# The lowest decay level of the HGRN scores, as products of neighbouring tokens summed by a matmul with ones

## The chip, the core and the metric

The kernel runs on one core of a Trainium2 chip, as one program. The metric is the device time of one execution in microseconds (us); the median of several runs counts. Engines are named as in the profile: TensorE (PE, its weight loads PEld), VectorE (DVE), ScalarE (ACT), GpSimd (POOL) and SyncE (SP), whose queue issues the DMAs.

## What is computed

The reference is one decoder layer over 512 tokens of 1024 channels, all in float32: a SwiGLU feed-forward network, a token mixer, and a second feed-forward network, each between two norms and with a residual. The mixer has four heads of HGRN2 and four of mLSTM. The change touches the scores of the HGRN heads. For one head with 128 channels, a query q, a key k = 1 - f and the logarithm of the forget gate f, the reference does, in each chunk:

```python
G = jnp.cumsum(gc, axis=2)
rel = G[:, :, :, None, :] - G[:, :, None, :, :]
decay = jnp.exp(jnp.where(causal, rel, -jnp.inf))
scores = jnp.sum(qc[:, :, :, None, :] * kc[:, :, None, :, :] * decay, axis=-1)
o = o_inter + jnp.einsum("bhts,bhsv->bhtv", scores, vc)
```

So the score of query t and key s is the sum over the channels of q_t k_s exp(G_t - G_s). For neighbours, t = s + 1, the decay is just f_t = 1 - k_t, and the score is the sum over the channels of q_t (1 - k_t) k_s.

## The kernel before

The tokens are held in four tiles of 128. The first feed-forward network runs, then the mixer, then the second network. TensorE does nearly all of its work in pieces that are queued so that something is always ready: in the mixer, `fill(n)` takes the next n steps of a queue of projections (`job_f` and `job_t`) and puts them between the steps of the HGRN and mLSTM parts. The projections multiply in a split form: each weight tile comes by DMA, ScalarE casts its high part (L208), VectorE makes the low part (L210), and three matmuls use them (L435, or L126 to L128).

Before the mixer's scores, `forget_gates` makes kk = 1 - f and the running sums G for two pairs of heads, `masks` lets GpSimd make the masks, the eye and the selectors, and ScalarE makes the queries q.

The scores are not made from the exponentials of G over a whole chunk, which would overflow, but by levels. `LEVELS` holds block sizes c = 1, 64, 32, 16, 8, 4, 2. At level c the 128 tokens of a chunk are cut into pairs of neighbouring blocks of c tokens; the queries of each second block meet the keys of the first. In `hgrn_level`, for c > 1, the queries are scaled by exp(G - ref) and the keys by exp(ref - G), with ref the G at the end of the first block (L996 to L1000). The scaled queries qe of the second blocks are packed to 512 columns for a pair of heads (2 heads of 4 chunks of 64 queries). For c = 1 no exponential is needed: L1002 makes 1 - kk of the odd tokens, that is f, and the keys are kk itself. L1005 multiplies the queries in. Then, at every level, eight matmuls (L1010), one for each head and chunk, take the 128 keys as weights and 64 columns of qe as the moving operand, and leave all scores of 128 keys by 64 queries in a PSUM bank. `copy_predicated` (L1014) takes from it the places that the level's mask allows, into sT.

`hgrn_levels` calls the levels for a pair of heads with their steps interleaved: level c = 1 comes first, before `hgrn_diag` (the scores of a token with itself, matmuls on L1050), then `hgrn_decays`, which takes the logarithm of kk in place (L958, so kk is used up) and makes H = G - log k there (L959), then the other levels. The keys of level c = 64, which is the second, need that H (L998, L1000). Pair 0 comes first, with six steps of the projections between two levels, then pair 1 with five, along with the gates of the mLSTM heads.

The order of the instructions on each engine is worked out when the program is built, by a planner that simulates the engines with durations of its own: it takes the earliest instruction in the program's order that is ready. On the chip each engine then goes through its queue in that order and waits where it must.

PSUM has eight banks, taken in turn by `ps()`; qe and the other work tiles of 512 columns come from four buffers (`st`).

Of the kernel before, what the change touches and what calls it, by code (L numbers as in the profile page):

```python
# [8 lines left out]
F32 = mybir.dt.float32  # L9
F32R = mybir.dt.float32r  # L10
AF = mybir.ActivationFunctionType
ALU = mybir.AluOpType
PSUM = bass.MemoryType.PSUM

P = 128
# [52 lines left out]
class Layer:  # L68
# [816 lines left out]
    def masks(self, mc, mb):  # L885

        nc = self.nc

        self.mask = mb.tile([P, len(LEVELS), 64], I32, name="mask")
        nc.gpsimd.memset(self.mask, 1)  # L890
        for n, c in enumerate(LEVELS):
            m = self.mask[:, n, :].rearrange("p (b c) -> p b c", c=c)
            pat = [[-2 * c, 64 // c], [0, c]]
            nc.gpsimd.affine_select(m, m, pattern=pat, compare_op=ALU.is_ge, fill=0.0, base=0, channel_multiplier=1)
            pat = [[2 * c, 64 // c], [0, c]]
            nc.gpsimd.affine_select(m, m, pattern=pat, compare_op=ALU.is_ge, fill=0.0, base=c - 1, channel_multiplier=-1)
        self.eye = mb.tile([P, P], I32, name="eye")
        nc.gpsimd.memset(self.eye, 1)
        nc.gpsimd.affine_select(
            self.eye, self.eye, pattern=[[1, P]], compare_op=ALU.is_equal, fill=0.0, base=0, channel_multiplier=-1  # L900
        )

        sel = mb.tile([4, 6, 2, 64], F32, tag="tmp", bufs=1, name="sel")
        nc.gpsimd.memset(sel, 1.0)
        self.sel = mc.tile([36, 6, P], F32R, name="selr")
        nc.gpsimd.memset(self.sel.bitcast(I32), 0)
        for n in range(6):
            pat = [[0, 2], [0, 64]] if n < 4 else [[-1, 2], [0, 64]]
            base = -n if n < 4 else -2 * (n - 4)
            nc.gpsimd.affine_select(  # L910
                sel[:, n], sel[:, n], pattern=pat, compare_op=ALU.is_equal, fill=0.0, base=base, channel_multiplier=1
            )
        for r in (0, 32):
            nc.gpsimd.tensor_copy(self.sel[r : r + 4], sel.rearrange("p n a b -> p n (a b)"))
# [69 lines left out]
    def hgrn_level(self, p, n, ke):  # L984

        nc = self.nc
        c = LEVELS[n]
        q, kk, G = self.q[p], self.kk[p], self.G[p]
        flat = lambda t: t.rearrange("p a t -> p (a t)")
        blk = lambda t: flat(t).rearrange("p (b two c) -> p b two c", two=2, c=c)  # L990
        qe = self.st("qe")
        qe3 = qe.rearrange("p (b c) -> p b c", c=c)
        if c > 1:
            el = self.st("el")
            el3 = el.rearrange("p (b c) -> p b c", c=c)
            ref = blk(G)[:, :, 0, c - 1 : c].broadcast_to([P, 512 // c, c])  # L996
            nc.vector.tensor_tensor(qe3, blk(G)[:, :, 1, :], ref, op=ALU.subtract)
            nc.vector.tensor_tensor(el3, ref, blk(kk)[:, :, 0, :], op=ALU.subtract)  # L998
            nc.scalar.activation(qe, qe, AF.Exp)
            nc.scalar.activation(blk(ke)[:, :, 0, :], el3, AF.Exp)  # L1000
        else:
            nc.vector.tensor_scalar(qe3, blk(kk)[:, :, 1, :], -1.0, 1.0, op0=ALU.mult, op1=ALU.add)  # L1002
            ke = kk
        yield
        nc.vector.tensor_tensor(qe3, qe3, blk(q)[:, :, 1, :], op=ALU.mult)  # L1005
        yield
        sc = self.ps()
        k8, q8 = flat(ke).rearrange("p (n s) -> p n s", s=P), qe.rearrange("p (n u) -> p n u", u=64)
        for m in range(8):
            nc.tensor.matmul(sc[:, 64 * m : 64 * m + 64], k8[:, m], q8[:, m], start=True, stop=True)  # L1010
        yield
        so = self.sT[:, 8 * p : 8 * p + 8, :].rearrange("p n (b two c) -> p n b two c", two=2, c=c)[:, :, :, 1, :]
        mk = self.mask[:, n : n + 1, :].broadcast_to([P, 8, 64]).rearrange("p n (b c) -> p n b c", c=c)
        nc.vector.copy_predicated(so, mk, sc.rearrange("p (n b c) -> p n b c", n=8, c=c))  # L1014
        yield
# [493 lines left out]
```

## Time and profile before

| what | value |
|---|---|
| median of 3 runs | 960.77 us (960.7 to 960.91) |
| the profiled execution | 960.65 us |
| its span, first to last instruction | 958.9 us |
| VectorE busy, 404 to 450 us | 37.83 of 46 us |
| VectorE busy, 450 to 457 us | 6.70 of 7 us |
| level c = 1, TensorE | from 400.8 us (pair 0) and from 454.2 us (pair 1) |

The profile is of one execution. Its page gives the busy time of each engine, the chain of waits that ended last and the costliest groups of instructions; further views give the instructions of one line, the instructions in order of time, and who waited for whom. In a timeline row stand the start in us, the duration in us, the engine, the line, the operation, what it writes and reads, and in brackets the idle time just before with what ended it. In a row of the chain in order of time stand the start, the duration, engine and tile, line, and a count. Matmuls overlap in the array, so the duration of one record is longer than the time by which the next one follows; the chain's rows give the latter.

### The profile page before, as it was taken

Reading aid. Unit: us, or ns where it says so; the run is one execution under the profiler, and the core shown is the slowest. Engines: PE = TensorE matmul, PEld = TensorE weight load, DVE = VectorE, ACT = ScalarE, POOL = GpSimd, SP = SyncE. Lnnn points to the kernel's source line nnn. Section 1 sums busy time; section 2 is a strip of 40 time slices with the busy share of each in tenths; the row PEclk is TensorE's granted clock in tenths of the full one; section 3 lists DMA queues with packets and bytes.
Section 4 is the critical chain, followed back from the end, with each engine's and each line's share of the span. In section 5 each row is a group of like instructions: output and inputs, shape, how many; then the busy total and the mean of one; then the engine's idle time right before and its main releaser. Section 6 shows DMA issues by size and latency. Waiting matters only on the chain.

```text
span 958.9 us, 15940 instructions
## 1 busy us (share of the span) xinstructions
PE 950.7 (99%) x6587; PEld 875.8 (91%) x6587; DVE 693.5 (72%) x860; ACT 467.2 (49%) x625; POOL 113.3 (12%) x160
## 2 busy tenths in 40 slices
PE   9999999999999999999999999999999999999997
PEld 7999999999888889998887888899999999988885
DVE  6799989987444476697846565797998899754543
ACT  7645444544434356855632444663454444543531
POOL 3530000000000035200001310344000000000001
PEclk9999999999999999999999999999999999999999
DMA  9244433244222024421312124324434332233202
GB/s 321 76 133 131 130 113 110 89 133 154 89 94 82 1 73 130 109 67 45 87 46 67 45 88 148 102 60 132 123 98 132 111 111 88 91 109 109 88 1 87
DMA packets 81666, 95.97 MB, mean 100 GB/s; under 512 B 4117, under 2 KB 61497, under 8 KB 81594
## 3 DMA queue, kind: packets, MB, share of 16 engines
q1 hardware_dynamic: 81306, 94.44, 31.7%
q8 instruction: 51, 0.84, 0.4%
q10 hardware_dynamic: 288, 0.52, 0.2%
q14 instruction: 21, 0.17, 0.1%
HBM read 92.85 MB, written 2.10 MB: 99 GB/s over the span
## 4 chain that ended last, share of the span: by engine, by line
PE 98%; issue 1%; ACT 0%; DMA 0%; POOL 0%; DVE 0%; DVEq 0%; POOLq 0%; ACTq 0%
PE ps L490 45%; PE ps L126 13%; PE ps L128 13%; PE ps L127 13%; PE ps L435 6%; PE ps L1010 3%; PE ps L269 1%; PE ps L445 1%; PE ps L1184 0%; PE ps L115 0%; PE ps L1095 0%; PE ps L1264 0%; PE ps L1291 0%; PE ps L1050 0%; PE ps L1288 0%
## 5 line engine op out<-in xcount | busy, mean ns | idle before, releaser
L208 ACT CAST w<-raw 128x1024 fp32r<-128x1024 f32 x214 | 225.3, 1054 | 322.8 <-PE ps L128 118.4
L210 DVE TENSOR_TENSOR w<-raw,w 128x1024 fp32r<-128x1024 f32 x214 | 268.9, 1259 | 123.6 <-ACT w L208 123.6
L490 PE MATMUL ps<-xq,w 128*128 128x256 f32 x2016 | 238.1, 277 | 0.0
L490 PEld LDWEIGHTS ps<-xq,w 128*128 128x128 f32 x2016 | 233.7, 188 | 0.2
L490 PE MATMUL ps<-sq,w 128*128 128x256 f32 x1440 | 171.0, 277 | 0.0
L490 PEld LDWEIGHTS ps<-sq,w 128*128 128x128 f32 x1440 | 167.4, 188 | 0.0
L128 PE MATMUL ps<-w,hs 128*128 128x512 f32 x336 | 131.0, 390 | 0.0
L126 PE MATMUL ps<-w,hs 128*128 128x512 f32 x336 | 130.9, 390 | 0.0
L127 PE MATMUL ps<-w,hs 128*128 128x512 f32 x336 | 130.8, 389 | 0.0
L126 PE MATMUL ps<-w,xq 128*128 128x512 f32 x208 | 84.9, 409 | 0.1
L128 PE MATMUL ps<-w,xq 128*128 128x512 f32 x208 | 81.1, 391 | 0.0
L127 PE MATMUL ps<-w,xq 128*128 128x512 f32 x208 | 81.1, 391 | 0.0
L224 DVE TENSOR_TENSOR raw<-raw,raw 128x1024 f32<-128x1024 f32 x64 | 80.0, 1251 | 0.7
L128 PEld LDWEIGHTS ps<-w,hs 128*128 128x128 f32 x336 | 63.1, 188 | 13.8 <-DVE hs L674 0.7
L127 PEld LDWEIGHTS ps<-w,hs 128*128 128x128 f32 x336 | 63.1, 188 | 12.8
L126 PEld LDWEIGHTS ps<-w,hs 128*128 128x128 f32 x336 | 63.1, 188 | 12.8
L356 POOL TENSOR_SCALAR col<-col 128x1 f32<-128x1 f32 x24 | 10.1, 422 | 500.6 <-ACT junk L355 500.4
L435 PE MATMUL ps<-xq,w 128*128 128x256 f32 x480 | 56.5, 278 | 0.0
L435 PEld LDWEIGHTS ps<-xq,w 128*128 128x128 f32 x480 | 55.5, 188 | 0.0
L674 DVE TENSOR_TENSOR hs<-hf,hs 128x1024 fp32r<-128x1024 f32 x42 | 51.2, 1218 | 0.0
L224 POOL TENSOR_TENSOR raw<-raw,raw 128x1024 f32<-128x1024 f32 x16 | 43.1, 2695 | 52.3 <-DVE w L210 43.0
L128 PEld LDWEIGHTS ps<-w,xq 128*128 128x128 f32 x208 | 39.0, 188 | 8.9 <-DVE xq L276 0.3
(231 smaller groups left out, 1015.4 us busy)
## 6 DMA issues: line engine op xcount, KB each, us to landing
raw<-in_ffn_w_in_dram SPq DMA_DIRECT2D x88, 512.0 KB, 4.4
raw<-in_ffn_w_out_dram SPq DMA_DIRECT2D x44, 512.0 KB, 3.8
raw<-in_w_mix_in_dram SPq DMA_DIRECT2D x28, 512.0 KB, 3.9
raw<-in_w_mix_out_dram SPq DMA_DIRECT2D x8, 512.0 KB, 3.7
out_dram<-xs SPq DMA_DIRECT2D x8, 256.0 KB, 2.1
xs<-in_x_dram SPq DMA_DIRECT2D x6, 256.0 KB, 6.4
gpost<-in_norm_post_dram SPq DMA_DIRECT2D x3, 512.0 KB
gpre<-in_norm_pre_dram SPq DMA_DIRECT2D x2, 512.0 KB, 4.1
```

Source lines behind the costliest of these rows:

```text
L126: mm(ps, sh, mh, start=start, stop=False, **kw)
L127: mm(ps, sh, ml, start=False, stop=False, **kw)
L128: mm(ps, sl, mh, start=False, stop=stop, **kw)
L208: nc.scalar.copy(hi, raw)
L210: nc.vector.tensor_tensor(lo, raw, hi.bitcast(F32), op=ALU.subtract)
L224: (nc.vector if late else nc.gpsimd).tensor_tensor(o, o, c, op=ALU.add)
L269: self.nc.tensor.transpose(pt[:, c * P : (c + 1) * P], src[:, k * P : (k + 1) * P], self.ident)
L356: nc.gpsimd.tensor_scalar(m, ss, s2 / D, b, op0=ALU.mult, op1=ALU.add)
L435: mm(ps[:, u0:u1], w[:, a, k, :], self.xop(k, b, u0, u1), start=k + n + m == 0, stop=k == ND - 1 and n == 2, skip_group_check=True,)
L490: self.nc.tensor.matmul(ps[:, c], wb[b][:, k, v], left[d][:, k, :], start=first and a + n + k == 0, stop=n == 2 and k == KH - 1, skip_grou ...
L674: self.nc.vector.tensor_tensor(t[:, 1], src, t[:, 0].bitcast(F32), op=ALU.subtract)
L1010: nc.tensor.matmul(sc[:, 64 * m : 64 * m + 64], k8[:, m], q8[:, m], start=True, stop=True)
```

## The change

For c = 1 alone, the packed queries are multiplied once more on VectorE, by the keys kk of the even tokens. Every column of qe then holds, for one pair of neighbours, the 128 channels' products q_t (1 - k_t) k_s. One matmul with a weight tile of ones sums them over the channels, and every one of the 128 output rows holds the same sum; the mask of the level takes the row that belongs to the key. The eight matmuls of this level go, for each of the two pairs, and so does the reading of kk by TensorE. The tile of ones is a new tile of 128 x 128, filled once by GpSimd ahead of the eye.

```diff
@@ masks
+        self.ones = mb.tile([P, P], F32, name="ones")
+        nc.gpsimd.memset(self.ones, 1.0)
         self.eye = mb.tile([P, P], I32, name="eye")
@@ hgrn_level
             nc.vector.tensor_scalar(qe3, blk(kk)[:, :, 1, :], -1.0, 1.0, op0=ALU.mult, op1=ALU.add)
-            ke = kk
         yield
         nc.vector.tensor_tensor(qe3, qe3, blk(q)[:, :, 1, :], op=ALU.mult)
+        if c == 1:
+            nc.vector.tensor_tensor(qe3, qe3, blk(kk)[:, :, 0, :], op=ALU.mult)
         yield
         sc = self.ps()
-        k8, q8 = flat(ke).rearrange("p (n s) -> p n s", s=P), qe.rearrange("p (n u) -> p n u", u=64)
-        for m in range(8):
-            nc.tensor.matmul(sc[:, 64 * m : 64 * m + 64], k8[:, m], q8[:, m], start=True, stop=True)
+        if c == 1:
+            nc.tensor.matmul(sc, self.ones, qe, start=True, stop=True)
+        else:
+            k8, q8 = flat(ke).rearrange("p (n s) -> p n s", s=P), qe.rearrange("p (n u) -> p n u", u=64)
+            for m in range(8):
+                nc.tensor.matmul(sc[:, 64 * m : 64 * m + 64], k8[:, m], q8[:, m], start=True, stop=True)
         yield
```

## The prediction

> **What bounds the kernel now.** I read the page's engine sums first, then the chain of waits, then what TensorE waited for.
>
> ```profile
> span 958.9 us, 15940 instructions
> PE 950.7 (99%) x6587; PEld 875.8 (91%) x6587; DVE 693.5 (72%) x860; ACT 467.2 (49%) x625; POOL 113.3 (12%) x160
> PE 98%; issue 1%; ACT 0%; DMA 0%; POOL 0%; DVE 0%; DVEq 0%; POOLq 0%; ACTq 0%
> PE ps L122 <- POOL ident masks.py:199: 1.5, 1, 1.5
> core 0: 958.9 us, clock 0.999
> ```
>
> TensorE is busy for 950.7 of 958.9 us, it makes up 98% of the chain that ended last, and the only wait of its matmuls that the view of waits shows is 1.5 us at the very start. So a stage's price is the time that its matmuls occupy TensorE, and work on the other engines is free until it makes TensorE wait. Of the 958.9 us only TensorE's can be saved by a change in the mixer.
>
> The change touches the lowest level (c = 1), once for each of the two head pairs. The chain in order of time shows both places, each between matmuls that fill TensorE around it:
>
> ```profile
> L1010 PE MATMUL ps<-qe,kk x32: 217/275/275, 400.8 to 455.8; 128*128 128x64 f32 x32
> 398.80 2.12 PE ps L435 x18
> 400.92 1.73 PE ps L1010 x16
> 402.65 10.65 PE ps L435 x90
> 451.20 1.78 PE ps L1050 x16
> 454.15 0.23 PE ps L128
> 454.38 1.73 PE ps L1010 x16
> 456.11 0.29 PE ps L126
> 456.40 0.23 PE ps L127
> ```
>
> The rows of L1010 that read kk are level c = 1: 8 matmuls of 64 columns in each pair, and 16 records, so an f32 matmul is recorded as two passes, each with its own weight load. One block takes 1.73 us. The first matmul after the block takes 0.29 instead of 0.23 us, so I count 1.73 + 0.06 = 1.79 us for the whole block, or 0.11 us a pass. L1050 just before it makes passes of 128 columns, and 16 of them take 1.78 us: 64 and 128 columns cost the same, 0.11 us. At this width the pass isn't bound by its columns but by the weight load beside it.
>
> **The change part by part.** *The matmuls.* Eight matmuls of 64 columns become one of 512 columns: the same 512 columns, but 2 weight loads in place of 16. A warm f32 pass of 512 columns is not in the trace. The nearest rows are these:
>
> ```profile
> 520.25 0.87 PE ps L1243 x4
> 521.12 0.23 PE ps L126
> L1243 PE MATMUL ps<-vm,kw 128*128 128x258 f32 x12 | 3.1, 380 | 0.0
> 2.87 3.78 PE ps L115 x4
> 8.22 1.89 PE ps L269 x8
> 21.24 0.87 PE ps L269 x8
> L115 PE MATMUL ps<-hf,one 1*128 1x512 f32 x4 | 3.8, 1096 | 0.1
> ```
>
> L1243 is f32 with 258 columns: 4 passes in 0.87 us, 0.2175 us each, twice the 0.11 us of 128 columns, so here the columns do decide, at 0.2175/258 = 0.84 ns a column. 512 columns give 0.43 us a pass, 0.86 us a matmul. The matmul behind L1243 takes its usual 0.23 us, so nothing is added at the exit. The second way to it is L115, an f32 matmul of 512 columns, but at the start of the program, where TensorE is slow: 3.78/4 = 0.945 us a pass. The same group of 8 transposes (L269) takes 1.89 us there and 0.87 us at 21 us; 0.945 x 0.87/1.89 = 0.435 us. Both ways agree on 0.43 us, and I take 0.86 us a matmul. The saving is 1.79 - 0.86 = 0.93 us a pair, **1.86 us** in both; if the 0.06 us at the exit stays, 1.74 us.
>
> The bounds of this price, by the rows however far: at worst the pass of L115 as it stands, 1.89 us a matmul, which is 0.10 us more than the block now, a loss of 0.2 us in all. At best the 0.23 us of L127, a pass of 512 columns of the other f32 type: 0.46 us a matmul, a gain of 2 x 1.33 = 2.66 us. I take 0.86 because L1243 has the same type, both operands of 128 partitions and a warm TensorE. The bounds give 958.1 and 961.0 us.
>
> The Trainium skill, page "TensorE: Matmul & The Clock Gate", Part 1, says that the array runs at half its clock until some 3.4 us of activity have passed. By that rule a pass of L115 would halve to 0.47 us and the saving would be 2 x (1.79 - 0.945) = 1.69 us, 959.1 us in all. The two rows of L269 agree with a halving (a factor of 2.2).
>
> *The products.* In each pair one more VectorE operation multiplies qe by every second column of kk. It has the shape and stride of the operation on L1005: 0.69 us, 2 x 0.69 = 1.4 us of VectorE time. It may run as soon as L1005 of this level is done:
>
> ```profile
> 390.76 0.69 DVE L1005 TENSOR_TENSOR qe<-qe,q 128x512 f32<-128x512 f32 x1 [0.69 <-ACT q L1365]
> 392.91 0.96 DVE L977 TENSOR_TENSOR qd<-q,qd 128x768 f32<-128x768 f32 x1 [1.47 <-ACT qd L964]
> 438.20 0.69 DVE L1005 TENSOR_TENSOR qe<-qe,q 128x512 f32<-128x512 f32 x1
> 440.43 0.71 DVE L1014 COPY_PREDICATED sT<-mask,ps 128x512 f32<-128x512 int32 x1 [1.54 <-PE ps L1010]
> ```
>
> In pair 0 VectorE is idle for 1.47 us behind it, in pair 1 for 1.54 us, and 0.69 us fits into either hole. The matmul of the level waits for the new product in place of the old one. That is ready at about 392.1 and 439.6 us, 8 and 14 us before TensorE reaches the place (400.9 and 454.4). So I cost it at nothing. Behind that matmul in TensorE's queue stand the projections (90 matmuls of L435 in pair 0), so a product later than that would stop all of TensorE. Without this cover it is 0.69 us in the chain of the next level, which is the first rival.
>
> *The ones.* GpSimd fills a tile of 128 x 128 ahead of the eye.
>
> ```profile
> masks.py:197 POOL MEMSET ident<- 128x128 f32 x1 | 0.2, 205 | 0.3 <-POOLq L1496 0.3
> 375.29 0.47 POOL L899 TENSOR_SCALAR_AFFINE_SELECT eye<-eye 128x128 int32<-128x128 int32 x1
> 386.47 0.73 POOL L904 MEMSET sel<- 4x768 f32 x1 [9.11 <-DVE G L946]
> ```
>
> The same fill costs 0.2 us at the start. What stands behind it in GpSimd's queue is late by 0.2 us: the rest of the masks and the eye, which is done at 375.8 us and first used after the matmuls of L1050 at about 397 us, then an idle stretch of 9.11 us. Nothing.
>
> *What is released.* The logarithm on L958 overwrites kk. Until now it had to wait for the matmuls of L1010, which read kk; afterwards only for those of L1050 and for a product long done:
>
> ```profile
> 402.73 1.28 ACT L958 ACT_TABLE_LOAD   x1 [1.38 <-PE ps L1010]
> 456.14 1.16 ACT L958 ACTIVATE kk<-kk,tiny 128x1024 f32<-128x1024 f32 x1 [0.58 <-PE ps L1010]
> 462.51 0.61 ACT L1000 ACTIVATE ke<-el 128x512 f32<-128x512 f32 x1
> 463.99 1.98 PEld L1010 LDWEIGHTS ps<-qe,ke 128*128 128x128 f32 x16
> 446.85 0.69 DVE L1005 TENSOR_TENSOR qe<-qe,q 128x512 f32<-128x512 f32 x1 [1.26 <-ACT qe L999]
> 461.07 1.22 DVE L210 TENSOR_TENSOR w<-raw,w 128x1024 fp32r<-128x1024 f32 x1
> ```
>
> ScalarE gets back up to 1.38 and 0.58 us of waiting. TensorE doesn't wait for it, so the gain is nothing, but it helps at the tightest place, which is level c = 64 of pair 1: its weights ke are ready at 462.51 + 0.61 = 463.1 us, and TensorE loads them at 463.99, a slack of 0.9 us. TensorE will come there 1.86 us earlier. Behind 446.85 us VectorE works without a break on what feeds ke; that backlog starts 0.93 us earlier, since it hangs on ScalarE's wait for TensorE behind pair 0. So 0.9 + 0.93 - 1.86 leaves about 0 us, and what L958 gains by its earlier release comes on top. I take no wait there.
>
> *The sum.* The profiled execution took 960.65 us, of which 958.9 are the span and 1.75 lie around it and stay. 960.65 - 1.86 = 958.79. The median of the runs, 960.77, lies 0.12 us higher: **958.9 us**.
>
> **The rivals.** *The next level comes too late.* If the order of work on VectorE puts the new product of pair 1 behind 446.85 us, into the stretch without a break, and that stretch doesn't move forward with TensorE, ke is late by 1.86 - 0.9 + 0.69 = 1.65 us, and the time is 960.55. For it speaks that the slack is small; against it the hole of 1.54 us at the product's natural place and ScalarE's earlier start.
>
> *Slower than before.* The order on each engine comes from a planner that sees other durations than before. If at the same place two splits of weights (L210, 1.22 us each) are also put ahead of what feeds ke, the delay is 1.65 + 2.44 = 4.1 us and the time 958.9 + 4.1 = 963.0. It decides from a delay of 1.86 us on, where the gain is gone. Against it: TensorE's order follows the program's here, and the splits have several buffers of cover.
>
> *The change doesn't save what it says.* If the weight loads had been hidden and only columns counted, equal columns would cost the same and nothing would be gained but the 0.12 us at the exits: 960.65, the same as 960.77. The equal price of passes of 64 and 128 columns speaks against it. The Trainium skill, same page, section "Back-to-back issue gap", counts an isolated matmul by its columns alone; the section adds that a stream of weight loads and matmuls is set by both, and the two rows, 1.73 and 1.78 us, side with that.
>
> *A cheaper pass.* At 0.23 us a pass the time is 958.1. Against it stands L1243.
>
> **How the numbers follow.** I call 0.2% (1.92 us, so 958.85 us) what a measurement can tell from no change. The forecast, with its own range of 958.7 to 959.1 (savings of 1.74 to 1.86 us, and 0.1 us to either side, since the runs lie between 960.7 and 960.91), gets 0.62. It lies on that border, and I divide it evenly. The late level gets 0.14, slower than before 0.10, nothing saved 0.05, the cheaper pass and anything else that gains 0.09. Faster by over 0.2%: 0.31 + 0.09 = 0.40, and 0.03 for smaller waits that close up around the blocks, taken from the even half: 0.43. Slower by over 0.2% (over 962.7): 0.08 of the 0.10. The rest, 0.49, is within 0.2%. The range goes from the cheaper pass to the dear one, 958.1 to 961.0, and leaves out the slower case and little else.
>
> **What would show it.** Two records of L1010 with 128x512 in each pair, about 0.43 us apart, where there were sixteen, 0.86 us for the block, and the matmul behind it at 0.23: if a pass takes 0.9 us, the price was wrong. Two more operations of VectorE at 0.69 us, inside the holes at about 391.5 and 438.9 us; if the second lies beyond 446 us, look for a wait of TensorE at level c = 64 of pair 1. No new wait of TensorE in the view of waits, and L958 no longer waiting for L1010. TensorE's busy time is to fall by as much as the span. A span that falls by less than TensorE's own work would say that the order of work changed, and the forecast would be wrong by what TensorE then waits.

## The result, and the profile after

The changed kernel takes 958.35 us (median of 11 runs, 957.67 to 958.93), beside 960.73 us for the kernel before (959.79 to 961.15). The ratio is 0.9977 with a 95% interval of 0.997 to 0.9985: faster by 0.15 to 0.30%. A second comparison gave 0.9981 (0.9972 to 0.9989). The profiled execution took 957.67 us.

The head of the page after:

```profile
span 956.0 us, 15884 instructions
PE 947.9 (99%) x6559; PEld 872.0 (91%) x6559; DVE 695.5 (73%) x862; ACT 466.6 (49%) x625; POOL 113.2 (12%) x161
PE 98%; issue 1%; ACT 0%; POOL 0%; DVE 0%; DVEq 0%; POOLq 0%; ACTq 0%
PE ps L122 <- POOL ident masks.py:199: 1.5, 1, 1.5
```

TensorE still sets the time. It has 28 passes fewer, its busy time fell by 2.8 us and the span by 2.9, and the fourth row, which is all that the view of waits has for its matmuls, is the one of before. VectorE has two instructions more and GpSimd one.

The changed level itself, from the group of matmuls of the new line (L1013) and the chain in order of time, where a row has start, duration, engine and tile, line and count:

```profile
L1013 PE MATMUL ps<-qe,ones 128*128 128x512 f32 x4 | 2.0, 591 | 0.0
397.77 2.12 PE ps L435 x18
399.90 0.86 PE ps L1013 x2
400.76 4.36 PE ps L435 x37
452.20 0.23 PE ps L128
452.43 0.86 PE ps L1013 x2
453.29 0.23 PE ps L126
```

Each block is two passes and 0.86 us long, where it was sixteen passes and 1.73 us, and the matmul behind it takes 0.23 us again, not 0.29.

So the two blocks saved 1.86 us. The profiled execution got faster by 2.98 us, and the chain shows where a good part of the rest lies. These are rows at the start and the end, first of the kernel before, then of the changed one:

```profile
10.12 0.85 PE ps L122 x4
12.50 8.74 PE ps L490 x72
946.97 0.24 PE ps L128
```

```profile
8.06 1.70 PE ps L269 x8
9.76 0.45 PE ps L122 x4
11.40 8.75 PE ps L490 x72
943.99 0.24 PE ps L128
```

The same four matmuls of L122 at 10 us took 0.85 us in one execution and 0.45 in the other: TensorE went to full speed in between. By the first matmul of L490 the second one is 1.10 us ahead, far before the mixer, in a part of the program that the change doesn't touch. From that matmul to the end of the chain's last one (TensorE works on for some 5 us behind it), the stretch is 947.21 - 12.50 = 934.71 us before and 944.23 - 11.40 = 932.83 us after, 1.88 us less. To the start of TensorE's very last matmul, at 952.26 and 949.28 us, the difference is 1.88 us as well. In the thirteen profiles of this study the first matmul of L490 starts between 11.40 and 12.69 us. I therefore compare the kernels by this stretch too, worked out in the same way for each. It isn't exact to the last tenth: from the first matmul of L490 to the first of the changed level, where TensorE's work is the same in all profiles but that of the diagonal, it takes 388.20 to 388.38 us, so two stretches can differ by 0.2 us without a reason in the mixer.

### The profile page after: what moved, and what is told of

It is laid out like the page before. It is cut to its first block, busy times and chain, and to the rows that moved or that the text cites. A ratio compares the mean times of both kernels' runs of the same rounds, so it can differ in the third digit from the quotient of the medians.

```text
span 956.0 us, 15884 instructions
## 1 busy us (share of the span) xinstructions
PE 947.9 (99%) x6559; PEld 872.0 (91%) x6559; DVE 695.5 (73%) x862; ACT 466.6 (49%) x625; POOL 113.2 (12%) x161
## 4 chain that ended last, share of the span: by engine, by line
PE 98%; issue 1%; ACT 0%; POOL 0%; DVE 0%; DVEq 0%; POOLq 0%; ACTq 0%
PE ps L490 45%; PE ps L126 13%; PE ps L128 13%; PE ps L127 13%; PE ps L435 6%; PE ps L1017 2%; PE ps L269 1%; PE ps L445 1%; PE ps L1191 0%; PE ps L1102 0%; PE ps L115 0%; PE ps L1298 0%; PE ps L1271 0%; PE ps L1057 0%; PE ps L122 0%
## 5 line engine op out<-in xcount | busy, mean ns | idle before, releaser
L490 PE MATMUL ps<-xq,w 128*128 128x256 f32 x2016 | 238.1, 277 | 0.0
L490 PEld LDWEIGHTS ps<-xq,w 128*128 128x128 f32 x2016 | 233.7, 188 | 0.2
L490 PE MATMUL ps<-sq,w 128*128 128x256 f32 x1440 | 171.0, 277 | 0.0
L490 PEld LDWEIGHTS ps<-sq,w 128*128 128x128 f32 x1440 | 167.4, 188 | 0.0
L435 PE MATMUL ps<-xq,w 128*128 128x256 f32 x480 | 56.8, 279 | 0.0
L435 PEld LDWEIGHTS ps<-xq,w 128*128 128x128 f32 x480 | 55.6, 188 | 0.5 <-issue 0.5
```

The costliest lines, as they stand in the source:

```text
L435: mm(ps[:, u0:u1], w[:, a, k, :], self.xop(k, b, u0, u1), start=k + n + m == 0, stop=k == ND - 1 and n == 2, skip_group_check=True,)
L490: self.nc.tensor.matmul(ps[:, c], wb[b][:, k, v], left[d][:, k, :], start=first and a + n + k == 0, stop=n == 2 and k == KH - 1, skip_grou ...
```

## The experiments

Theory 1 is the prediction's: a pass on TensorE costs the larger of its weight load and its columns, and the gain is the weight loads that went. Theory 2 was that the earlier release of kk, or a better order of work behind it, makes up part of the gain. The medians of the changed kernels are of 5 to 11 runs.

| kernel | median us | ratio to before (95%) | stretch us | against before |
|---|---|---|---|---|
| before | 960.4 to 960.7 | | 934.71 | |
| the change | 958.35 | 0.9977 (0.997 to 0.9985) | 932.83 | -1.88 |
| the change again | 958.44 | 0.9981 (0.9972 to 0.9989) | 932.88 | -1.83 |
| eight matmuls with ones | 960.71 | 1.0003 (0.9994 to 1.0011) | 934.75 | +0.04 |
| four matmuls with ones | 958.14 | 0.9976 (0.9968 to 0.9985) | 932.73 | -1.98 |
| pair 0 alone | 959.56 | 0.9992 (0.9982 to 1.0001) | 933.88 | -0.83 |
| product alone | 960.34 | 0.9999 (0.9991 to 1.0008) | 934.76 | +0.05 |
| fourteen products more | 962.22 | 1.002 (1.0011 to 1.0029) | 936.07 | +1.36 |
| diagonal with ones | 958.24 | 0.9977 (0.9967 to 0.9986) | 932.68 | -2.03 |
| 64 keys at c = 64 | 957.09 | 0.9964 (0.9951 to 0.9978) | 931.85 | -2.86 |
| split product | 958.16 | 0.9978 (0.9968 to 0.9988) | 932.61 | -2.10 |
| 128 - c keys | 956.38 | 0.9956 (0.9944 to 0.9969) | 930.45 | -4.26 |
| both | 955.99 | 0.9954 (0.9942 to 0.9967) | 930.47 | -4.24 |

**The change again.** No edit.

> The changed kernel once more, to see how much of the 2.4 us is the change. Theory 1 (TensorE's passes): two blocks of 0.86 us in place of 1.79, a gain of 1.86 us, and every further difference between two executions comes from the start, where TensorE goes to full speed at a varying time: from the first matmul of L490 to the last of the kernel this run is 1.9 us shorter than the profile of before, whatever the whole time is. Theory 2 (the logarithm of kk is released earlier, and the order of work behind it is better): some 0.5 us more is gained between the blocks, so the same stretch is 2.3 us or more shorter.

The stretch is 1.83 us shorter than before, and the first matmul of L490 starts at 12.47 us, as late as in the profile of before. Theory 1 holds, and nothing is left for theory 2.

**Eight matmuls with ones.** It keeps the product, the ones and the release of kk, and takes back the merging alone.

```diff
-            nc.tensor.matmul(sc, self.ones, qe, start=True, stop=True)
+            for m in range(8):
+                nc.tensor.matmul(sc[:, 64 * m : 64 * m + 64], self.ones, qe[:, 64 * m : 64 * m + 64], start=True, stop=True)
```

> As the changed kernel, with the product and the ones, but eight matmuls of 64 columns with ones as weights in place of one of 512. Theory 1: sixteen passes of 0.11 us again, 1.79 us a block, so the gain is gone: within 0.3 us of the kernel before. Theory 2 (the gain comes from kk being free for the logarithm earlier): the release is kept, so the gain of about 2 us is kept.

The gain is gone, in the median (960.71) and in the stretch (+0.04 us). The chain shows the old block, with other operands:

```profile
399.08 2.12 PE ps L435 x18
401.20 1.73 PE ps L1014 x16
402.93 1.11 PE ps L435 x9
```

So neither the release nor the order behind it gains anything by itself. Theory 2 falls.

**Four matmuls with ones.** The same with 128 columns each.

> As the changed kernel, but four matmuls of 128 columns with ones. Theory 1: a pass costs the larger of a weight load (0.11 us) and its columns (0.84 ns each, 128 columns are 0.11 us): eight passes, 0.89 us a block, so the gain is nearly whole: 1.8 us faster than before. A rival, that each weight load adds to its pass (0.05 us a load on top of the columns): 8 x 0.05 + 0.86 = 1.26 us a block, 1.1 us faster than before.

```profile
398.38 2.12 PE ps L435 x18
400.50 0.89 PE ps L1014 x8
401.39 2.62 PE ps L435 x23
```

0.89 us a block, as theory 1 has it to the hundredth; loads that add to their passes would have made 1.26. The load is hidden from 128 columns on. The whole gain comes from passes of 64 columns that were shorter than their load. Here the block decides, not the stretch: the 90 passes of L435 behind the block of pair 0 took 10.21 us in this run, where they take 10.60 us with the change. The two runs with the split product, further down, show the same 10.21 us, and no run shows why.

**Pair 0 alone.** The condition `c == 1` becomes `c == 1 and p == 0`, with `ke = kk` for the other pair.

> The change in pair 0 alone; pair 1 keeps eight matmuls with kk. Theory 1: half the gain, 0.93 us; one block of 0.86 and one of 1.79 us. Theory 2: pair 1 is where VectorE is without a break, and the release counts there: clearly less than half of the gain.

The stretch is 0.83 us shorter, a little under half (it would be 0.94 of 1.88), and the 0.1 us that is missing was lost before the level began (it starts 388.38 us after the first matmul of L490, and 388.26 us before the change). The median's 0.8 us, with an interval that just touches 1, says the same with less sharpness. Theory 2's imbalance doesn't show.

**The product alone.** The kernel before, with the new operation writing into a tile that isn't read.

```diff
         nc.vector.tensor_tensor(qe3, qe3, blk(q)[:, :, 1, :], op=ALU.mult)
+        if c == 1:
+            s3 = self.st("scr").rearrange("p (b c) -> p b c", c=c)
+            nc.vector.tensor_tensor(s3, qe3, blk(kk)[:, :, 0, :], op=ALU.mult)
```

> The kernel before with the new product added, into a work tile that nobody reads; the eight matmuls with kk stay. It prices the product by itself. Theory 1 (the product is covered): no change, within 0.3 us of the kernel before, and from the first matmul of L490 to the last of the kernel within 0.1 us of before. Rival: 0.69 us a pair shows on TensorE, up to 1.4 us slower.

No change: 960.34 us, and +0.05 us in the stretch. The product is covered.

**Fourteen products more.** In pair 1, ahead of the one that is needed; they write into a work tile that isn't read.

```diff
+            s3 = self.st("scr").rearrange("p (b c) -> p b c", c=c)
+            for _ in range(14 if p else 0):
+                nc.vector.tensor_tensor(s3, qe3, blk(kk)[:, :, 0, :], op=ALU.mult)
             nc.vector.tensor_tensor(qe3, qe3, blk(kk)[:, :, 0, :], op=ALU.mult)
```

> The changed kernel with fourteen more products in pair 1, ahead of the one that is needed, into a work tile that nobody reads: 9.5 us more of VectorE, and about 4 us of it fit into its idle times there. It looks for the point from which a late product costs something. Rival of the prediction (a product in the stretch without a break stops TensorE): the level's matmul is about 4 us late and the kernel loses 4 us against the changed one, some 2 us slower than before. Theory 1 in its present form: the planner sees that VectorE is late and puts projections in front of the level's matmul (39 in the built program, where there were 6), so TensorE finds other work and the time stays within 0.5 us of the changed kernel, 1.4 to 2.2 us faster than before.

My present form of theory 1 was wrong here, and the rival of the prediction right: 962.22 us, 1.8 us slower than before and 3.2 us slower than the change by the stretch. The view of waits (who waited for whom: us in total, times, longest) has what the changed kernel doesn't have:

```profile
PE ps L1016 <- DVE qe L1012: 2.4, 1, 2.4
PE ps L1020 <- ACT ke L1002: 0.3, 1, 0.3
```

L1012 is the needed product, at 462.5 us. The planner did put 39 projections ahead of the level's matmul, but on the chip these ran out 2.4 us too early. The two waits make 2.7 of the 3.2 us. The cover of a product in pair 1 is real, and it is limited.

**The diagonal with ones.** The same rewriting for the scores of a token with itself; `self.kes[1]` is a work tile for keys.

```diff
-            for c in range(NT):
-                s = slice(c * P, (c + 1) * P)
-                nc.tensor.matmul(sc[:, s], self.kk[p][:, a, s], self.q[p][:, a, s], start=True, stop=True)
+            dg = self.kes[1][:, a]
+            nc.vector.tensor_tensor(dg, self.kk[p][:, a], self.q[p][:, a], op=ALU.mult)
+            nc.tensor.matmul(sc, self.ones, dg, start=True, stop=True)
```

> The changed kernel, and the same way for the scores of a token with itself: eight matmuls of 128 columns become two products and two matmuls of 512 columns with ones. Theory 1 (a pass costs the larger of its weight load, 0.11 us, and its columns): 16 passes of 0.11 us, 1.78 us, become 4 of 0.43 us, 1.72 us, so next to nothing is gained beyond the change, 0.1 us, though twelve weight loads a pair go. Rival (weight loads add to their passes, 0.05 us each): 12 x 0.05 = 0.6 us a pair, 1.2 us beyond the change.

```profile
396.75 1.72 PE ps L1058 x4
398.46 2.06 PE ps L435 x18
```

1.72 us, where sixteen passes of 128 columns took 1.78. Twelve weight loads less a pair, and next to nothing gained: the stretch is 0.15 to 0.2 us shorter than with the change alone, which is within its scatter. It is the sharpest counterpart to the change. The trick is the same; what differs is whether the columns or the load set the pass.

**64 keys at c = 64.** Here the keys that the mask lets through are the first 64 of a chunk, so the weights can be cut to them.

```diff
+                r = P - c if c == 64 else P
-                nc.tensor.matmul(sc[:, 64 * m : 64 * m + 64], k8[:, m], q8[:, m], start=True, stop=True)
+                nc.tensor.matmul(sc[:r, 64 * m : 64 * m + 64], k8[:, m, :r], q8[:, m], start=True, stop=True)
...
+        r = P - c if c == 64 else P
-        nc.vector.copy_predicated(so, mk, sc.rearrange("p (n b c) -> p n b c", n=8, c=c))
+        nc.vector.copy_predicated(so[:r], mk[:r], sc.rearrange("p (n b c) -> p n b c", n=8, c=c)[:r])
```

> The changed kernel, and at level c = 64 only the 64 keys that the mask lets through are loaded as weights (64 columns in place of 128; their 64 output rows are the ones that are read). Columns and count of the matmuls stay. Theory 1, with the load's time in proportion to its columns: a pass is 0.055 us, a block 0.9 us in place of 1.79, 1.8 us in both pairs beyond the change, so 3.6 us faster than before. Rival, that a pass has a floor of 0.11 us whatever it loads: nothing beyond the change, 1.9 us faster than before.

The gain beyond the change is 1.0 us in the stretch (932.83 to 931.85), not 1.8. The first two rows are of the changed kernel, the others of this one:

```profile
411.36 1.73 PE ps L1017 x16
413.09 0.66 PE ps L983 x6
```

```profile
411.78 1.07 PE ps L1018 x16
412.86 0.81 PE ps L983 x6
```

The block fell from 1.73 to 1.07 us, so there is no floor of 0.11 us a pass. It did not reach 0.9, and the transposes behind it take 0.15 us more. Within the block the passes follow each other by 0.058 us, close to the 0.055 expected; what is lost is lost at its borders. Probably the short passes no longer hide the full weight load that follows, but no run tests that. The direction of theory 1 holds; its size ignored the borders of the block.

**The split product.** The product's high and low part, two matmuls of the faster type; `onesr` is the tile of ones, cast once to that type by GpSimd.

```diff
+            hi, lo = (self.sp.tile([P, 512], F32R, tag="st", bufs=4, name=self.nm("hl")) for _ in range(2))
+            nc.scalar.copy(hi, qe)
+            nc.vector.tensor_tensor(lo, qe, hi.bitcast(F32), op=ALU.subtract)
...
-            nc.tensor.matmul(sc, self.ones, qe, start=True, stop=True)
+            nc.tensor.matmul(sc, self.onesr, hi, start=True, stop=False)
+            nc.tensor.matmul(sc, self.onesr, lo, start=False, stop=True)
```

> The changed kernel, with the product split into a high and a low part (one more copy on ScalarE, one more subtraction on VectorE, in each pair) and summed by two matmuls with ones of the faster f32 type. If a pass of 512 columns of that type takes 0.23 us as in the projections, a block is 0.46 us in place of 0.86: 0.8 us beyond the change, 2.7 us faster than before, and from the first matmul of L490 to the last 2.7 us less. Rival: the two added operations come too late in pair 1, where VectorE is without a break; then the gain beyond the change is 0.4 us or less and TensorE waits at this level.

The block is as short as hoped, the time is not. These rows are from the chain, then from the waits of the weight loads, then from the instructions in order of time:

```profile
400.33 0.23 PE ps L1018
400.56 0.23 PE ps L1019
```

```profile
PEld ps L1023 <- ACT ke L1004: 0.8, 1, 0.8
```

```profile
459.71 1.06 ACT L974 ACTIVATE ek<-ek 128x1024 f32<-128x1024 f32 x1 [1.32 <-DVE ek L973]
460.68 0.61 ACT L1004 ACTIVATE ke<-el 128x512 f32<-128x512 f32 x1
```

0.46 us a block, a gain of 0.8 us in both, but the stretch is only 0.22 us shorter than with the change, although the 90 passes of L435 behind the block of pair 0 were 0.39 us quicker too. The weight load now waits 0.8 us, and TensorE itself 0.4 us, for ke of the second level in pair 1, the place that the prediction named as the tightest. Counted from the first matmul of L490, ke is ready at 461.29 - 11.80 = 449.49 us, 0.97 us later than with the change (459.92 - 11.40 = 448.52): the work of ScalarE and VectorE came later, not only TensorE earlier. The rival was right in the size, and the two added operations are the likely cause; the wait came one level behind the one that it named.

**128 - c keys at four levels**, `c > 4` in place of `c == 64` above.

> The changed kernel, with 128 - c keys loaded as weights at the levels c = 64, 32, 16 and 8 (64, 96, 112 and 120 columns; the rows left out are masked). If a pass takes what its load takes, in proportion to the columns, and each block pays 0.25 us for its two borders as the block of 64 keys did, then c = 64 gains 0.5 us a pair, c = 32 some 0.2 us, c = 16 and c = 8 nothing or a little less than nothing: 1 to 1.5 us beyond the change, 2.9 to 3.4 us faster than before. Rival, no cost at the borders: 0.9 + 0.45 + 0.22 + 0.11 us a pair, 3.3 us beyond the change.

```profile
412.19 1.07 PE ps L1018 x16
413.26 0.80 PE ps L983 x6
414.07 4.11 PE ps L435 x36
418.17 1.33 PE ps L1018 x16
419.50 4.30 PE ps L435 x36
423.80 1.53 PE ps L1018 x16
```

It gained 2.4 us beyond the change in the stretch (932.83 to 930.45), between the two expectations. Loads of 64, 96 and 112 columns make blocks of 1.07, 1.33 and 1.53 us, beside 1.73 for 128; 120 columns make 1.63. Less the 0.15 us that the transposes behind c = 64 take more, this adds up to 1.2 us a pair, the whole gain. From 96 columns up a block grows by 0.0125 us a column, and by that line 64 columns would make 0.93 us, so only that block pays more at its borders, 0.14 us within it and 0.15 us behind. Inside the blocks, from the start of one matmul to the next, the passes are 58, 85, 98 and 105 ns apart for loads of 64, 96, 112 and 120 columns, and 112 ns for 128: 0.83 ns a column.

**Both**: the split product, and 128 - c keys at c = 64 and 32.

> The split product and the shorter loads at c = 64 and 32 together. If they add up: 0.8 us and 1.0 to 1.5 us beyond the change, 3.7 to 4.2 us faster than before, 956.2 to 956.7 us. Rival: TensorE, earlier by 4 us, meets keys of pair 1 that are not ready, and part of it goes into waits at level c = 64 of pair 1.

955.99 us, 4.4 us faster than before. In the stretch it is as short as the shorter loads at four levels (930.47 and 930.45 us), but it shortens the loads at two of them only. By their blocks the other two, c = 16 and c = 8, are worth 0.20 + 0.10 us a pair, 0.6 us in both, so the split product brought some 0.6 us here (an estimate), where alone it brought 0.22. The wait for ke of 0.8 us is in its view of waits too. Part of the split's gain isn't its own block: the 90 passes of L435 behind the block of pair 0 take 10.21 us here too, 0.39 us less than with the change, and that isn't explained.

## Why the prediction was right

**The price of the block.** Predicted 0.86 us in place of 1.79, measured 0.86, in both pairs. Of the two ways to it, the pass of 258 columns held. The slow pass at the start gave the same by luck: L115's matmuls start 0.85 us apart once they run (at 4.74 and 5.59 us), so the 0.945 us held waits, and the 1.89 us of L269 held some too; the two nearly cancel. By the spacing of the transposes, 213 ns at the start and 110 ns later, 0.85 us becomes 0.44. The 959.1 us that the prediction got from half of 0.945 us was too high for the same waits. The reason held as well: passes of 64 columns were set by their weight load (eight matmuls with ones lost the gain, four kept it).

**The product.** It was covered (product alone: +0.05 us), but not as I had placed it. VectorE around it, in the changed kernel:

```profile
389.74 0.69 DVE L1006 TENSOR_TENSOR qe<-qe,q 128x512 f32<-128x512 f32 x1 [0.69 <-ACT q L1372]
390.47 1.20 DVE L1009 TENSOR_TENSOR qe<-qe,kk 128x512 f32<-128x512 f32 x1
391.90 0.96 DVE L979 TENSOR_TENSOR qd<-q,qd 128x768 f32<-128x768 f32 x1 [0.24 <-ACT qd L966]
436.25 0.69 DVE L1006 TENSOR_TENSOR qe<-qe,q 128x512 f32<-128x512 f32 x1
438.48 0.72 DVE L1021 COPY_PREDICATED sT<-mask,ps 128x512 f32<-128x512 int32 x1 [1.54 <-PE ps L1017]
439.10 0.68 DVE L1009 TENSOR_TENSOR qe<-qe,kk 128x512 f32<-128x512 f32 x1
441.01 1.22 DVE L210 TENSOR_TENSOR w<-raw,w 128x1024 fp32r<-128x1024 f32 x1 [0.64 <-ACT w L208]
```

Before, the idle time behind the copy was this:

```profile
442.96 1.23 DVE L210 TENSOR_TENSOR w<-raw,w 128x1024 fp32r<-128x1024 f32 x1 [1.24 <-ACT w L208]
```

In pair 0 the product lies in the hole, but takes 1.20 us, not 0.69. In pair 1 the planner put it behind the copy on L1021, so the hole of 1.54 us stayed empty, and the product took 0.6 us out of the next idle time (1.24 before, 0.64 now). Both places were idle enough.

**The ones.** No wait appeared behind them.

**The release of kk, and the tightest place.** L960 (the former L958) no longer waits for TensorE. I had reckoned the slack of ke at level c = 64 of pair 1 as about nothing, plus what the earlier release would give. It became larger than before:

```profile
459.31 0.61 ACT L1002 ACTIVATE ke<-el 128x512 f32<-128x512 f32 x1
461.12 1.98 PEld L1017 LDWEIGHTS ps<-qe,ke 128*128 128x128 f32 x16
```

ke is ready at 459.9 us and loaded at 461.1, 1.2 us. The release paid here as cover, not as time: with eight matmuls of ones, which keep the release and give up the gain, ke is ready at 462.15 us and loaded at 464.27, a slack of 2.1 us, and with pair 0 alone, where pair 1 keeps its old form, at 462.22 and 463.08, 0.9 us as before the change. That this place binds next was right: the split product and the fourteen products both ran into a wait for ke.

**The rivals.** A late level was no part of the change. Fourteen products made the kernel slower than before, mostly through the product itself (2.4 us), which the prediction had as the danger to the projections behind the matmul, and only 0.3 us through ke, the path of the two rivals. The loads were not hidden, and the pass was not cheaper.

**The sum.** 1.86 us was predicted, the medians differ by 2.38 us, with an interval of 1.4 to 2.9, and by 1.94 us in the repetition. The median of 958.35 us lies below the forecast's narrow range of 958.7 to 959.1, and nearer to the 958.1 of a cheaper pass than to 958.9; only the 0.86 us of the block in the trace tells the two apart. The stretch, which leaves the start out, says 1.88 and 1.83. The half microsecond more in the first comparison is within its interval; that it is the start's scatter is likely, since the start varied by 1.3 us between profiles, but the starts of the timed runs weren't recorded. The prediction's border of 0.2% lies inside the interval, as the even split of the chances had it.

## What to carry to other kernels

Where TensorE is the bound, count a small matmul by the larger of its weight load and its columns in each pass: merging pays while the columns are shorter than the load (64 columns here) and stops paying where they are equal (128, as on the diagonal). The same rule finds the larger gain of this kernel: load fewer weight columns where a mask throws the rows away. And once TensorE has become faster, look for the operand with the least slack before gaining more; here a further 0.8 us in two blocks, at the price of more work ahead of that operand, bought 0.2.

## What the runs showed of the hardware

**The start scatters by more than half of the effect.** TensorE went to full speed between 9.5 and 12.4 us after the start (its transposes go from 213 to 110 ns, from one start to the next), and the first matmul of L490 began between 11.40 and 12.69 us with an unchanged program up to there. The Trainium skill, page "TensorE: Matmul & The Clock Gate", Part 1, says that the window which decides on the clock runs freely and doesn't start with the kernel, so that the change varies by about 500 ns to either side. That it varies agrees; by how much doesn't, since 9.5 to 12.4 us is nearly three times that spread. The granted clock in the profile reads 1.00 from the start on and doesn't show it; the rows of L122 do.

**A product was held up by GpSimd.** In pair 0 it took 1.20 us instead of 0.69, while GpSimd made its casts:

```profile
387.83 3.28 POOL L916 CAST selr<-sel 4x768 fp32r<-4x768 f32 x2
```

The casts end at 391.11 us and the product at 391.67, about 0.55 us later, the better part of its usual time. The Trainium skill, page "SBUF — State Buffer", section "SBUF: two separate sides", says that VectorE and GpSimd share one pair of ports under an exclusive lock, which a VectorE operation with two SBUF inputs needs against a GpSimd operation that reads SBUF. These rows agree with it, and so do those of pair 0 alone, where the same casts and operations fell in another order:

```profile
388.87 2.58 POOL L916 CAST selr<-sel 4x768 fp32r<-4x768 f32 x2
388.87 1.89 DVE L210 TENSOR_TENSOR w<-raw,w 128x1024 fp32r<-128x1024 f32 x1 [2.50 <-ACT w L208]
390.79 1.21 DVE L1007 TENSOR_TENSOR qe<-qe,q 128x512 f32<-128x512 f32 x1
392.03 0.69 DVE L1010 TENSOR_TENSOR qe<-qe,kk 128x512 f32<-128x512 f32 x1
```

There the two operations beside the casts took 1.89 and 1.21 us instead of 1.22 and 0.69, the casts 2.58 us instead of 3.28, and the product, which starts after their end at 391.45 us, its usual 0.69 us. So it was the cast beside it that made the product slow.

**Weight loads by columns.** The Trainium skill, page "TensorE: Matmul & The Clock Gate", section "LDWEIGHTS (loading the stationary operand)", gives the load as columns divided by 1.2, in nanoseconds: 0.83 ns a column. The 0.83 ns a column between the passes with 64 to 128 columns agree; the block of 64 columns shows in addition what its borders cost.
